# Four estimates of the issue planner change in a one-core RWKV-7 / Conformer inference step

## The chip, the cores and the metric

The kernel runs on one core of one Trainium2 chip. The metric is the device time of one execution in microseconds (us), lower is better. A core has five engines, each with its own list of instructions that it takes in order: TensorE (PE in the profile; PEld are its weight loads), VectorE (DVE), ScalarE (ACT), GpSimd (POOL) and SyncE (SP), which here issues the DMA transfers between HBM and the on-chip memory.

## The reference

One layer over 512 latent tokens and 128 context tokens with 1024 channels, all in float32. What is computed, cut to its core:

```python
mod = silu(cond) @ ada_w + ada_b                # 6 x 1024 columns, for the two conditions c and c_ctx
sh1, sc1, g1, sh2, sc2, g2 = split(mod, 6)
xn = rmsnorm(x, norm1_g) * (1 + sc1) + sh1
rkv, glu_in, gate_r, gate_c = split(xn @ w_in)  # 1536 + 1024 + 1024 + 1024 columns
y_r = rwkv7(rkv, xn)       # 8 heads, a forward and a backward scan over the tokens,
                           # plus bonus = sum(r * kd * r_k) * v, group norm, gate, @ w_out_rwkv
y_c = conv_branch(glu_in)  # GLU, depthwise conv of width 31, LayerNorm, swish, @ w_out_conv
merged = sigmoid(gate_r) * y_r + sigmoid(gate_c) * y_c
x = x + g1 * (merged @ w_o)
xn2 = rmsnorm(x, norm2_g) * (1 + sc2) + sh2
x = x + g2 * (relu(xn2 @ mlp_w1) ** 2 @ mlp_w2)
y = rmsnorm(x, final_g)    # also returned: the context's final scan states
```

## The kernel before

All 640 tokens lie along the free dimension, the channels on the 128 partitions. Every dense product is split in three: weights and activations are each held as a high and a low part in a 32-bit format that TensorE multiplies fast, and `mm3` adds high x high, high x low and low x high. The weights come as float32 blocks of 256 KB; ScalarE makes the high part, GpSimd (or VectorE) the low part.

The kernel has three stages. A set-up makes the modulation columns 0 to 15 (shift and scale of the first norm), the first norm and the low-rank inner products; it takes the first 55 us. Then comes one long stage, up to somewhat past 700 us, in which everything between the two norms is interleaved: the projections, the scans, the convolution, the gates and the branch outputs, and the modulation columns 16 to 47, called late here. The last stage is `w_o`, the second norm and the MLP.

The order in the long stage is planned while the program is built. Each strand of work is a Python generator, a lane: `solve`, `scan`, `side` and `prep` for each of four pairs of heads, the weight splitter, `lora2_all`, `ada_all`, `conv_all` and others. Each has an urgency in `URGENT`. A clock `now` runs on the estimated time of TensorE; `free` holds the estimated time at which VectorE, ScalarE and GpSimd are through with what has been issued. Their instructions go through `Timed`, which adds an estimate made by `cost_v`, `cost_a` or `cost_g`, and notes the estimated end in `last`. A lane runs until it yields. A number means: wake me so many microseconds of planned time from now. Nothing (or "T") means: wake me 0.2 us (`SEM`) after the estimated end of what I issued last. A letter means: wake me when that engine is nearly free. Whenever no lane may run, the filler issues one more dense product (`fill`, from the list `todo`). What comes out is a fixed order for TensorE, VectorE and ScalarE; the order of DMAs on SyncE and of instructions on GpSimd is set by the framework's own scheduler, which goes by its own timeline and issues what is ready.

The places that the change touches:

- `ada_late` and `ada` make one late column of the modulation: 1024 x 128 weights come in two halves of 256 KB into one buffer (`adl`, a single one, allocated in `adl_load`, L620). `ada_late` yields `GAP_ADA`, `ada` multiplies the first half (four products on bank `ad`), yields the pause in question, multiplies the second half, and two small products and two ScalarE instructions end the column. As there is one buffer, the second load can start only when the products of the first half have read it. `ada_all` goes through 32 columns with the urgency 4, next to the last. The pause is also used in the set-up, by the early columns.
- `root` raises a statistic to the power -0.5 on GpSimd; `inv_norm` calls it and then, on a plain yield, multiplies the result out on TensorE. In the long stage that is eight times with 10 columns (twice for each pair of heads) and twice with 3.
- `inverse` transposes 128 x 1024 elements in 32 x 32 blocks on VectorE, three times for each pair of heads; TensorE's products on the second and third result follow.
- `operands` ends with two VectorE instructions that leave the operand of the bonus in `kk`; the lane then marks the pair as prepared, and `side` calls `bonus`, whose products (`bsum`, bank `t`) read `kk`.

`calm` is an empty list during the set-up and holds one element from then on.

Of the kernel before, what the change touches and what calls it, by code (L numbers as in the profile page):

```python
# [13 lines left out]
ALU = mybir.AluOpType  # L14
# [46 lines left out]
LEAD, SEM, LOAD = 0.40, 0.2, 4.0  # L61
# [1 line left out]

URGENT = dict(scan=0, split=0.3, shift=1.45, post=1, side=0.9, solve=1, prep=1.5, lora=2, ada=4, out=4.5, branch=0.5, conv=1.6)

GAP_LORA, GAP_ADA = 1.5, 3.5
V_STEP = 20
GLU_AT = 12
TICK, ENTRY, QUOTA, CREDIT, STAY, DEBT = 3.413, 3060, 1.55, 700, 350, 6000
# [7 lines left out]
def hybrid_step(ctx: ExitStack, tc: tile.TileContext, I, O):  # L77
# [32 lines left out]
    def aps_(kw, *names):  # L110
        return sum(hasattr(kw.get(k), "shape") for k in names)

    def cost_v(name, n, src, kw):
        return 0.07 + 0.06 * aps_(kw, "scalar", "scalar1") + n / (480 if name == "tensor_tensor_scan" else 960)

    def cost_a(name, n, src, kw):
        return (0.08 if src[0].space == PSUM else 0.16) + 0.093 * aps_(kw, "scale", "bias") + n / 1400

    def cost_g(name, n, src, kw):
        return 1.9 if kw.get("op") == ALU.pow else 0.26 + n / (450 if name == "tensor_tensor" else 960)  # L120

    V, A, G = Timed(nc.vector, "V", cost_v), Timed(nc.scalar, "A", cost_a), Timed(nc.gpsimd, "G", cost_g)

# [6 lines left out]
    def bank(tag="mm"):  # L130
        return pp.tile([P, 512], F32, name="ps_" + tag, tag=tag, bufs=2 if tag == "mm" else 1)

    def st(shape, tag, bufs=1, dt=F32):
        return sb.tile(shape, dt, name=tag + "_t", tag=tag, bufs=bufs)
# [4 lines left out]
    def wt(shape, tag, bufs=1, dt=F32):  # L139
        return wk.tile(shape, dt, name=tag + "_w", tag=tag, bufs=bufs)  # L140

    def ldtmp():
        pool, n, cols = tmp_pool[-1]
        return pool.tile([P, cols], F32, name="tmp", tag="tmp", bufs=n)
# [16 lines left out]
    def pc(name, i, n=1):  # L161
        return par[:, PCOL[name] + i:PCOL[name] + i + n]
# [29 lines left out]
    def mm(out, lhsT, rhs, start=True, stop=True, **kw):  # L192
        PE.matmul(out=out, lhsT=lhsT, rhs=rhs, start=start, stop=stop, **kw)  # L193
        cyc = math.prod(rhs.shape[1:]) * (1 if rhs.dtype == F32R else 2 if "is_transpose" in kw else 4)
        m = math.prod(lhsT.shape[1:])
        overlap = 128 // m if m < 128 else 128 // rhs.shape[0]
        cols = cyc * rhs.shape[0] / 128 * (1 if rhs.dtype == F32R else 0.5)
        gated["cols"] += cols
        gated["burst"] -= cols
        gated["credit"] = min(gated["credit"] + cols, CREDIT)  # L200
        kind = (m, rhs.shape[0], rhs.dtype)
        if kind != gated["kind"]:
            advance(now[0] + SWITCH * gated["drain"] / (2400 if gated["warm"] else 1200))
        gated.update(kind=kind, drain=0 if rhs.dtype == F32R else max(cyc, 256) - max(cyc / overlap, 64))
        advance(now[0] + (max(cyc / overlap, 64) + EXTRA) / (2400 if gated["warm"] else 1200))
        ready[out.name] = ("P", now[0] + SEM / 2)
        last[0] = now[0]
# [7 lines left out]
    planner, calm = [lambda: None], []  # L215
# [142 lines left out]
    def inv_norm(src, scale, op, c, tg, bc):  # L358


        ps = bank(tg[0])
        for i in range(5):
            mm(ps[:, 2 * i:2 * i + 2], src[:, P * i:P * i + P], hsel)
        r = st([P, 10], "rh", 2)
        root(r, ps[:, 0:10], scale, op, c)
        yield
        for tag, a, b in ((tg[1], 0, 4), (tg[2], 4, 5)):
            pb = bank(tag)
            for i in range(a, b):
                for j in range(2):  # L370
                    mm(pb[64 * j:64 * j + 64, P * (i - a):P * (i - a) + P], r[:, 2 * i + j:2 * i + j + 1].to_broadcast([P, 64]),
                       ident)
            bc(P * a, P * b, pb[:, 0:P * (b - a)])
# [9 lines left out]
    def ada(cols, tag, raws):  # L383

        n = len(cols) * P
        ps = bank(tag)
        for k0, k1, raw in raws:
            for k in range(k0, k1):
                g = 32 * (k % 4)
                mm(ps[g:g + 32, 0:n], csb[:, 2 * k:2 * k + 32], raw[:, k - k0, :], k < 4, k >= 4, tile_position=(0, g))  # L390
            yield 2.5 if k0 == 0 else 0.0
        e = ldtmp()[:, 0:n]
        A.activation(e, ps[:, 0:n], AF.Copy)
        yield
        for i, col in enumerate(cols):
            mm(ps[:, n + 2 * i:n + 2 * i + 2], e[:, i * P:(i + 1) * P], sel)
        for i, col in enumerate(cols):
            A.activation(mod[:, col, :], ps[:, n + 2 * i:n + 2 * i + 2], AF.Identity, bias=pc("ada_b", col))
# [113 lines left out]
    def dram(name):  # L512
        if name not in spill:
            spill[name] = dr.tile([P, T], F32, name=name, tag=name)
        return spill[name]
# [146 lines left out]
    def operands(p):  # L662

        gr = grp[p]
        gr["Dc"] = wt([P, NY], "Dc", 2)
        r, k = rk[0, p], rk[1, p]

        def load(d):
            th, at = st([P, T], "tA"), st([P, T], f"ath{d}")
            DMA.dma_start(out=th, in_=dram(f"z0{d}{p}"))  # L670
            DMA.dma_start(out=at, in_=dram(f"z1{d}{p}"))
            return th, at

        loaded = load(0)
        t0 = st([P, T], "pt0")
        A.activation(t0, k, AF.Square, scale=pc("k_k", p))
        kk = gr["kk"] = st([P, T], "kk")
        yield
        yield from inv_norm(t0, 1.0, "max", 1e-24, ("t",) * 3,
                            lambda a, b, ps: V.scalar_tensor_tensor(out=kk[:, a:b], in0=k[:, a:b], scalar=pc("k_k", p),  # L680
                                                                    in1=ps, op0=ALU.mult, op1=ALU.mult))
        ath = []
        for d in range(2):
            ys = slice(20 * d, 20 * d + 20)

            def tv(ap):
                return (ap[:, ::-1] if d else ap).rearrange("p (y t) -> p y t", t=C32)


            th, at = loaded  # L690
            ath.append(at)
            A.activation(th, th, AF.Copy, bias=1.0)
            yield "T"
            cs = st([P, 20, C32], "tB")
            csf = cs.rearrange("p y t -> p (y t)")
            for a, b in HALVES:
                V.tensor_tensor_scan(out=csf[:, a:b], data0=smask, data1=th[:, a:b], initial=0.0,
                                     op0=ALU.mult, op1=ALU.add)
                yield "V"
            if d == 0:  # L700
                loaded = load(1)
            yield "T"
            A.activation(E[:, :, 1:33], cs, AF.Exp, scale=-0.5 * CDEC)
            yield "A"
            A.activation(cs, cs, AF.Exp, scale=0.5 * CDEC)
            yield "A"
            if d == 0:
                while p and (3 not in rates or (p > 1 and p - 2 not in chained)):
                    yield 0.2
                ARGH = gr["ARGH"] = st([P, 2, NY, 64], "ARGH", 2)  # L710
            A.activation(gr["Dc"][:, ys].unsqueeze(2), E[:, :, 32:33], AF.Copy)
            V.tensor_tensor(out=ARGH[:, 0, ys, 0:32], in0=tv(kk), in1=E[:, :, 0:32], op=ALU.mult)
            yield "V"
            V.tensor_tensor(out=ARGH[:, 0, ys, 32:64], in0=tv(r), in1=E[:, :, 1:33], op=ALU.mult)
            DMA.dma_start(out=ARGH[64:128, 1, ys, :], in_=ARGH[64:128, 0, ys, :])
            yield "V"
            if d == 0:
                while p and turned[p - 1] < 3:
                    yield 0.2
                BK = gr["BK"] = wt([P, NY, 64], "BK")  # L720
            bc, kc = (0, 32) if d == 0 else (32, 0)
            t1 = st([P, T], "pt0")
            V.scalar_tensor_tensor(out=t1, in0=at, scalar=1.0, in1=kk, op0=ALU.add, op1=ALU.mult)
            yield "V"
            V.scalar_tensor_tensor(out=BK[:, ys, bc:bc + 32], in0=tv(t1), scalar=-0.5, in1=cs,
                                   op0=ALU.mult, op1=ALU.mult)
            yield "A"
            A.activation(at, at, AF.Identity, scale=ka2[:, p:p + 1], bias=ka2[:, 4 + p:5 + p])
            yield "T"
            V.tensor_tensor(out=at, in0=at, in1=k, op=ALU.mult)  # L730
            yield "V"
            V.tensor_tensor(out=BK[:, ys, kc:kc + 32], in0=tv(at), in1=cs, op=ALU.mult)
            yield "V"
        operated.add(p)
        V.tensor_tensor(out=kk, in0=ath[0], in1=ath[1], op=ALU.add)
        yield "V"
        V.scalar_tensor_tensor(out=kk, in0=kk, scalar=pc("r_k", p), in1=r, op0=ALU.mult, op1=ALU.mult)
        yield SEM

    BKt = wt([P, 2, NY, 64], "BKt")  # L740
    for s in range(2):
# [908 lines left out]
```

## Time and profile before

| | |
|---|---|
| median of 3 runs | 1296.28 us (1286.36 to 1297.65) |
| the profiled execution | 1300.42 us, its span 1298.6 us |
| TensorE busy | 1228.2 us, 95% of the span |
| VectorE, ScalarE, GpSimd busy | 56%, 42%, 12% |
| mean granted TensorE clock | 0.958 of full speed |
| moved by DMA | 140.43 MB, mean 108 GB/s |

The span reaches from the first to the last instruction of the profiled execution; 1.8 us of its time lie outside. TensorE's busy share counts time in which products run, at whatever clock; matmuls are pipelined and their ends are modelled. [...]

### The profile page before, as it was taken

To read this page: it belongs to the slowest core of one execution; us is meant where nothing else is said; L and a number is where in the kernel's file an instruction comes from. 1 tells how busy PE (TensorE), PEld (TensorE's weight loads), DVE (VectorE), ACT (ScalarE), POOL (GpSimd) and SP (SyncE) were. 2 spreads that over 40 slices of the span, in tenths; PEclk is the share of its full clock that TensorE was granted. 3 is DMA by queue.
4 is the path that set the end of the run, shared out by engine and by line. 5 is a ranking of instruction groups with operands and counts; after the bars stand their busy time and mean duration, and the time that the engine had idled before them with its cause. 6 is when DMAs were issued, how large, how long until landed. Compare 5 with 4: busy or idle time off the path is not lost.

```text
span 1298.6 us, 31716 instructions
## 1 busy us (share of the span) xinstructions
PE 1228.2 (95%) x13362; PEld 1092.9 (84%) x13362; DVE 720.9 (56%) x1446; ACT 548.8 (42%) x1390; POOL 152.4 (12%) x112
## 2 busy tenths in 40 slices
PE   8988899998999899999979999999999999999996
PEld 5776676777677776777979999999999999999996
DVE  5525576747557766877953365664433443444344
ACT  5545466634555565465225123354421431342130
POOL 1122120112011100122413310000000000000000
PEclk9998999968799989999989999999999999999998
DMA  9445433113222522343413853112222222222222
GB/s 370 151 158 175 143 109 114 59 43 119 77 94 68 153 92 70 116 126 93 136 58 121 270 195 125 49 50 82 72 75 81 67 82 74 74 82 69 78 74 82
DMA packets 82575, 140.43 MB, mean 108 GB/s; under 512 B 17024, under 2 KB 31616, under 8 KB 82432
## 3 DMA queue, kind: packets, MB, share of 16 engines
q1 hardware_dynamic: 82432, 138.39, 33.2%
q8 instruction: 105, 1.72, 0.6%
q14 instruction: 38, 0.31, 0.1%
HBM read 113.52 MB, written 22.22 MB: 105 GB/s over the span
## 4 chain that ended last, share of the span: by engine, by line
PE 82%; DVE 7%; DMA 6%; issue 2%; ACT 1%; SPq 0%; POOL 0%; POOLq 0%; DVEq 0%; ACTq 0%
PE ps_mm L193 43%; PE ps_b L193 24%; PE ps_t L193 7%; PE ps_a L193 6%; DMA adl_w<-in_adal 3%; PE ps_ad L193 3%; DVE BK_w L106 2%; DVE cacc_w L106 1%; DMA adar_s<-in_adaw 1%; DVE vS_w L106 1%; DVE ARGH_t L106 1%; DMA u_t<-gate 1%; DMA svu_w<-in_st 0%; DVE kk_t L106 0%; DVE svu_w L106 0%
## 5 line engine op out<-in xcount | busy, mean ns | idle before, releaser
L193 PE MATMUL ps_mm<-xh_t,wh_t 128*128 128x320 f32 x584 | 198.2, 339 | 0.9 <-ACT tmp L106 0.9
L193 PE MATMUL ps_mm<-xh_t,wl_t 128*128 128x320 f32 x584 | 198.8, 340 | 0.0
L193 PE MATMUL ps_mm<-xl_t,wh_t 128*128 128x320 f32 x584 | 196.7, 337 | 0.0
L106 ACT ACTIVATE wh_t<-wr_t 128x512 fp32r<-128x512 f32 x135 | 84.9, 629 | 143.2 <-PE ps_b L193 108.4
L106 POOL TENSOR_TENSOR wl_t<-wr_t,wh_t 128x512 fp32r<-128x512 f32 x63 | 85.0, 1350 | 462.0 <-ACT wh_t L106 418.0
L106 ACT ACTIVATE svu_w<-ps_a 64x128 f32<-64x128 f32 x320 | 87.0, 272 | 122.9 <-PE ps_a L193 117.3
L193 PEld LDWEIGHTS ps_mm<-xh_t,wl_t 128*128 128x128 f32 x584 | 117.0, 200 | 10.8 <-issue 7.2
L193 PEld LDWEIGHTS ps_mm<-xl_t,wh_t 128*128 128x128 f32 x584 | 116.7, 200 | 9.6 <-issue 6.1
L193 PEld LDWEIGHTS ps_mm<-xh_t,wh_t 128*128 128x128 f32 x584 | 116.3, 199 | 9.6 <-issue 4.3
L106 DVE SCALAR_TENSOR_TENSOR cacc_w<-upad_w,par_t,cacc_w 128x640 f32<-128x640 f32 x90 | 88.6, 984 | 4.3 <-ACT cacc_w L106 2.1
L106 DVE TENSOR_TENSOR wl_t<-wr_t,wh_t 128x512 fp32r<-128x512 f32 x72 | 49.7, 690 | 56.2 <-ACT wh_t L106 56.2
L106 ACT ACTIVATE tmp<-ps_mm 128x320 f32<-128x320 f32 x80 | 34.9, 436 | 98.9 <-PE ps_mm L193 90.4
L193 PE MATMUL ps_mm<-ARGH_t,wh_t 128*128 128x320 f32 x284 | 74.8, 308 | 0.0
L106 DVE TENSOR_TENSOR svu_w<-ps_b,Dc_w 64x128 f32<-64x128 f32 x152 | 43.7, 288 | 54.5 <-PE ps_b L193 51.0
L106 POOL TENSOR_TENSOR rt_t<-rt_t,mhalf_t 128x3 f32<-128x3 f32 (+1 forms) x7 | 6.5, 921 | 532.0 <-DVE rt_t L106 532.0
L193 PE MATMUL ps_mm<-ARGH_t,wl_t 128*128 128x320 f32 x212 | 65.8, 310 | 0.0
L106 ACT ACTIVATE mwh<-wr_t 128x512 fp32r<-128x512 f32 x49 | 31.0, 632 | 71.1 <-PE ps_b L193 66.8
L106 DVE SCALAR_TENSOR_TENSOR ARGH_t<-ps_mm,mod_t,ARGH_t 128x320 f32<-128x320 f32 (+2 forms) x45 | 22.6, 511 | 59.9 <-PE ps_mm L193 59.9
L106 DVE TENSOR_TENSOR tmp<-tmp 128x320 f32<-128x320 f32 x64 | 31.2, 489 | 43.8 <-ACT tmp L106 43.7
L106 DVE TENSOR_TENSOR mwl<-wr_t,mwh 128x512 fp32r<-128x512 f32 x49 | 33.8, 690 | 34.9 <-ACT mwh L106 34.9
L193 PEld LDWEIGHTS ps_mm<-ARGH_t,wh_t 128*128 128x128 f32 x284 | 50.4, 188 | 0.0
L106 ACT ACTIVATE BKt_w<-ps_a 32x512 f32<-32x512 f32 (+3 forms) x80 | 39.9, 503 | 19.9 <-PE ps_a L193 18.9
(372 smaller groups left out, 3226.2 us busy)
## 6 DMA issues: line engine op xcount, KB each, us to landing
wr_t<-in_w SPq DMA_DIRECT2D x214, 256.0 KB, 2.7
adl_w<-in_adal SPq DMA_DIRECT2D x64, 256.0 KB, 3.0
adar_s<-in_adaw SPq DMA_DIRECT2D x16, 512.0 KB, 8.4
ARGH_t<-in_x SPq DMA_DIRECT2D x8, 640.0 KB, 6.9
z<-tmp SPq DMA_DIRECT2D x32, 160.0 KB, 3.0
gate<-tmp SPq DMA_DIRECT2D x32, 160.0 KB, 2.2
tA_t<-z SPq DMA_DIRECT2D x8, 320.0 KB, 3.1
ath_t<-z SPq DMA_DIRECT2D x8, 320.0 KB, 3.3
```

The source lines that it names most:

```text
L106: return f(*args, **kw)
L193: PE.matmul(out=out, lhsT=lhsT, rhs=rhs, start=start, stop=stop, **kw)
```

## The change

Four estimates of the planner change; every instruction and every operand stays. `GAP_ADA` goes from 3.5 to 4.5, and the pause between the two halves of a late column, 2.5 before, becomes `GAP_ADA` too (in the set-up it stays 2.5). A block transpose on VectorE is counted with 520 elements per microsecond in place of 960, a power on GpSimd with 2.6 us in place of 1.9. At the end of `operands` the lane yields nothing in place of `SEM`: it wakes 0.2 us after the estimated end of its last instruction, not 0.2 us after issuing it.

```diff
-GAP_LORA, GAP_ADA = 1.5, 3.5
+GAP_LORA, GAP_ADA = 1.5, 4.5
@@ cost_v
-        return 0.07 + 0.06 * aps_(kw, "scalar", "scalar1") + n / (480 if name == "tensor_tensor_scan" else 960)
+        return 0.07 + 0.06 * aps_(kw, "scalar", "scalar1") + n / (480 if name == "tensor_tensor_scan" else 520 if name == "transpose" else 960)
@@ cost_g
-        return 1.9 if kw.get("op") == ALU.pow else 0.26 + n / (450 if name == "tensor_tensor" else 960)
+        return 2.6 if kw.get("op") == ALU.pow else 0.26 + n / (450 if name == "tensor_tensor" else 960)
@@ ada
-            yield 2.5 if k0 == 0 else 0.0
+            yield (GAP_ADA if calm else 2.5) if k0 == 0 else 0.0
@@ operands
         V.scalar_tensor_tensor(out=kk, in0=kk, scalar=pc("r_k", p), in1=r, op0=ALU.mult, op1=ALU.mult)
-        yield SEM
+        yield
```

## Rows read from the trace of the kernel before

**Rows 1.** The page's busy times: us (share of the span) xinstructions.
```profile
PE 1228.2 (95%) x13362; PEld 1092.9 (84%) x13362; DVE 720.9 (56%) x1446; ACT 548.8 (42%) x1390; POOL 152.4 (12%) x112
```

**Rows 2.** TensorE's waits, whole span: us in total, times, longest.
```profile
PE ps_ad L193 <- DMA adl_w<-in_adal: 17.0, 9, 2.9
PE ps_t L193 <- DVE kk_t L106: 7.5, 8, 1.8
```

**Rows 3.** The waits of TensorE's weight loads, whole span.
```profile
PEld ps_ad L193 <- DMA adl_w<-in_adal: 19.5, 10, 3.1
```

**Rows 4.** Timeline (start, us; in brackets the idle before): the five longest such waits.
```profile
64.72 0.16 PEld L193 LDWEIGHTS ps_ad<-adl_w,csb_t 128*32 128x32 f32 x8 [2.33 <-DMA adl_w<-in_adal]
77.62 0.20 PEld L193 LDWEIGHTS ps_ad<-adl_w,csb_t 128*32 128x32 f32 x8 [2.81 <-DMA adl_w<-in_adal]
112.00 0.20 PEld L193 LDWEIGHTS ps_ad<-adl_w,csb_t 128*32 128x32 f32 x8 [2.55 <-DMA adl_w<-in_adal]
328.03 0.20 PEld L193 LDWEIGHTS ps_ad<-adl_w,csb_t 128*32 128x32 f32 x8 [3.14 <-DMA adl_w<-in_adal]
454.82 0.16 PEld L193 LDWEIGHTS ps_ad<-adl_w,csb_t 128*32 128x32 f32 x8 [2.28 <-DMA adl_w<-in_adal]
```

**Rows 5.** Timeline: first halves and SyncE's loads behind them; the lane's last product.
```profile
59.67 0.16 PEld L193 LDWEIGHTS ps_ad<-adl_w,csb_t 128*32 128x32 f32 x8 [0.18 <-issue]
60.59 0.45 SPq L620 DMA_DIRECT2D adl_w<-in_adal  x1
...
321.29 0.16 PEld L193 LDWEIGHTS ps_ad<-adl_w,csb_t 128*32 128x32 f32 x8
324.64 0.81 SPq L620 DMA_DIRECT2D adl_w<-in_adal  x1
...
552.17 0.16 PEld L193 LDWEIGHTS ps_ad<-adl_w,csb_t 128*32 128x32 f32 x8
```

**Rows 6.** SyncE's waits, whole span: us in total, times, longest.
```profile
SPq L620 <- PE ps_ad L193: 102.7, 36, 8.9
```

**Rows 7.** Stretches: us, busy of five engines (instructions), granted clock, DMA share, GB/s.
```profile
76.00:84.00 8.00, 6.38 (x37) 5.32 (x38) 0.00 (x0) 3.32 (x9) 1.34 (x2) 0.79 0.41 132
112.00:124.00 12.00, 11.33 (x55) 9.14 (x56) 6.24 (x9) 5.19 (x12) 1.35 (x1) 0.58 0.32 102
144.00:152.00 8.00, 6.94 (x76) 5.17 (x77) 4.95 (x7) 2.37 (x8) 0.00 (x0) 0.79 0.24 83
...
324.00:344.00 20.00, 17.12 (x189) 13.31 (x189) 8.99 (x17) 8.63 (x27) 2.60 (x2) 0.57 0.27 74
456.00:464.00 8.00, 8.00 (x137) 6.80 (x140) 5.39 (x12) 4.86 (x13) 0.00 (x0) 0.57 0.28 85
260.00:288.00 28.00, 26.02 (x271) 19.07 (x271) 13.39 (x52) 9.68 (x25) 3.23 (x2) 0.57 0.12 39
```

**Rows 8.** The chain that ended last: runs of dense products, start, us, count.
```profile
118.08 5.37 PE ps_mm L193 x21
...
775.67 3.52 PE ps_mm L193 x24
```

**Rows 9.** Timeline: a slower power and the products that read it.
```profile
540.83 2.52 POOL L106 TENSOR_TENSOR rh_t<-rh_t,mhalf_t 128x10 f32<-128x10 f32 x1 [3.25 <-DVE rh_t L106]
544.10 0.85 PEld L193 LDWEIGHTS ps_t<-cst_t,rh_t 128*64 128x64 f32 x16
```

**Rows 10.** Timeline: a block transpose and the products on its result.
```profile
168.84 2.21 DVE L106 STREAM_TRANSPOSE Gt_w<-Nb_w 128x1024 f32<-128x1024 f32 x1
171.97 0.76 PEld L193 LDWEIGHTS ps_t<-Gt_w,Gf_w 32*32 32x32 f32 x80 [0.19 <-issue]
```

**Rows 11.** Timeline: the bonus's operand and the products on it.
```profile
219.04 0.88 DVE L106 SCALAR_TENSOR_TENSOR kk_t<-kk_t,par_t,rS_w 128x640 f32<-128x640 f32 x1
220.75 0.20 PEld L193 LDWEIGHTS ps_t<-kk_t,cst_t 128*64 128x64 f32 x4 [0.73 <-ACT Y_w L106]
```

**Rows 12.** Timeline: the store of the last gate.
```profile
711.50 0.38 SPq L611 DMA_DIRECT2D gate<-tmp  x1
```

## The prediction

> **What bounds the kernel now.** I read the page's busy shares first: TensorE works 95% of the span [rows 1], so its instruction list, which it takes strictly in order, is what the time is made of. A changed order can bring time in two ways only: less idling between products, or a higher granted clock while they run.
>
> Second, the waits by engine: of what TensorE waited for, the largest item is the late modulation's weight load, 17.0 us in 9 waits; next come waits on VectorE's kk, 7.5 us in 8 [rows 2]. The same loads seen from the weight-load side are 19.5 us in 10 waits [rows 3]. The reader should see that these stalls are few and long and belong to one lane.
>
> Third, the timeline at those waits: the five longest (2.28 to 3.14 us) stand in [rows 4]. Each is at the second half of a column: the column at 59.67 multiplies its first half, its second load is issued at 60.59 when the one buffer is free, and the second half starts at 64.72 after 2.33 us of nothing [rows 4, 5]. The planner put 2.5 us between the halves; the load took 4.13 us from issue to product. At 321.29 it was worse: the first half's products ran, and SyncE came to the next load only at 324.64 [rows 5]. So 2.5 us is too little for two reasons, the transfer and the queue ahead of it.
>
> Fourth, the granted clock by stretch [rows 7]. Right behind six of the late loads the mean clock is 0.57 to 0.79, though TensorE is busy again. [...] The six stretches (a third of the 0.79 kind, 196 to 204, is like the two shown) give 3.4 + 10.1 + 3.4 + 3.4 + 17.2 + 6.9 = 44.4 us at half clock. Another, 260 to 288, has 24.1 us of it and no late load: half clock has other causes too.
>
> **The change, part by part.** No instruction is added or removed; only the place of instructions in the lists of TensorE, VectorE and ScalarE moves, and with them the places that SyncE's and GpSimd's own instructions find.
>
> *Gap between the halves, 2.5 to 4.5 us.* It puts 2 us more of other products between the halves of each of 32 columns. The load does not move with it: it is issued when the buffer is free (60.59, less than a microsecond after the products at 59.67 began [rows 5]), not when the lane wakes. So every wait shrinks by 2 us. Of the five listed, 0.33 + 0.81 + 0.55 + 1.14 + 0.28 = 3.1 us stay; the other five waits together are 19.5 - 13.1 = 6.4 us, 1.3 on average, and I take them as gone. Removed: 16.4 of 19.5 us on the weight-load side; on TensorE's own account the same share of 17.0 us, 14.3 us. Bounds: nothing, if SyncE comes to the load later by the same 2 us, and 17.0 us.
>
> *Gap before a column, 3.5 to 4.5 us.* All late loads belong to second halves, so this removes no wait: 0. Together the two gaps make the lane up to 32 x 3.0 = 96 us longer. Its last product load is at 552.17 [rows 5]; it would end by about 650. Cover: dense gate products run until the last gate is stored at 711.50 [rows 12], so no engine waits for the lane, and its results are first read after the loop. If that cover is gone, a column alone costs about 13 us, as between the second halves of the first two columns, at 64.72 and 77.62 [rows 4].
>
> *SyncE behind the load.* While SyncE stands at such a load for the buffer it can issue nothing else: 102.7 us in 36 waits already [rows 6]. Queued behind are weight loads, for which ScalarE and GpSimd would wait and then TensorE. None of that reaches TensorE today (no such row among its waits), and the blocking depends on when the first half ends, not on the gap. I take 0; the bound on the other side is that weights come late as often as the modulation's did, 17.0 us [rows 2], which takes the first gap's gain away again.
>
> *GpSimd's power, 1.9 to 2.6 us.* It moves the products that read the power 0.7 us later, eight times. One of the slower powers took 2.52 us, ended at 543.35, and its products came at 544.10 with no wait noted [rows 9]. So there is nothing to remove: 0, bounds 0 and plus or minus 8 x 0.7 = 5.6 us if the cover of dense products failed.
>
> *Block transposes, 1.14 to 2.04 us as planned.* The trace has 2.21 us for the one at 168.84, and TensorE's products on its result, at 171.97, show 0.19 us of ordinary issue time [rows 10]. No wait to remove: 0. The planner will think VectorE busy 0.9 us longer, 12 times, and place up to 10.8 us of other VectorE work later; VectorE is at 56% [rows 1], so that is the bound against the change, and I take 0.
>
> *End of the bonus's operand.* The lane now wakes when the operand is done and not 0.2 us after it was issued. At 219.04 the operand took 0.88 us, to 219.92; TensorE's product on it came at 220.75 after 0.73 us of waiting, put down to ScalarE's reading of the shared bank [rows 11]. The operand was done before that wait began, so I take 0; bounds 0 and 4 x 0.88 = 3.5 us. The 7.5 us of kk waits [rows 2] are mostly the second use of one bank by the same lane without a pause, which stays.
>
> *The clock.* The same kind of dense product comes every 3.52 / 24 = 0.147 us at full clock and every 5.37 / 21 = 0.256 us in the half-clock stretch behind the wait at 112.00 [rows 8]. So a microsecond at half clock loses 1 - 0.147/0.256 = 0.43 us, and the 44.4 us lose 19.0 us. How much comes back the rows don't settle: six late loads have such a stretch behind them, four have none, and 260 to 288 fell without one [rows 7]. Between 0 and 19.0 us I take the middle, 9.5 us.
>
> [...]
>
> The sum goes against the profiled execution: span 1298.6, time 1300.4 us, which is 4.1 us above the median of the runs shown (1286.4 to 1297.7). 1300.4 - 14.3 - 9.5 = 1276.6, so 1277 us, 1.5% under the median.
>
> **The rivals.**
>
> *The clock is not won back.* The late loads go, but the clock falls at other places of the new order. For it: 24.1 us at half clock with no late load. Against it: six of the late loads are followed by it directly. Time: 1300.4 - 14.3 = 1286.
>
> *The load stays as late.* SyncE reaches the load 2 us later because the order ahead of it has grown. For it: 324.64 [rows 5]. Against it: 60.59, at once when the buffer was free. Time: 1300, no change; with the clock's spread 1291 to 1301.
>
> [...]
>
> *Slower: half clock during a scan.* Moving modulation columns to later places leaves the scan's small products with less beside them, and the clock stays at half as from 260 to 288, which lies in the first scan. Price 0.43 us per us; three more stretches like that one (72 us at half clock) cost 31 us: 1286 + 31 = 1317. It decides for slower when the loss passes 1309 - 1286 = 23 us, that is 54 us more at half clock than the profiled run has without its late loads. For it: that stretch exists. Against it: nothing in the change touches the scan's own gaps.
>
> *Slower: the lane outlasts the loop.* It would have to slip 160 us, to beyond 711.50; the gaps give at most 96. Each column left over costs 13 us, so two of them decide.
>
> **How the numbers follow.** A measurement of this kernel can tell about 1% from no change: 1283 to 1309 counts as the same. Forecast (1264 to 1283, waits gone and part of the clock back): 0.55. Clock not won back (1283 to 1291): 0.18. Load as late as before (1291 to 1301): 0.12. Half clock in a scan: 0.12, lane outlasts the loop: 0.03, both above 1309. Hence faster 0.55, same 0.30, slower 0.15. The likeliest case's own range is 1264 (all 36.0 us of both terms) to 1283. The range to hold 8 in 10 reaches down to 1260, since other runs shown lie up to 14 us under the profiled one, and up to 1301, where 0.15 is left out above and some 0.05 below.
>
> **What would show it.** Right: waits on the late modulation's weights under 4 us in total; its last product between 580 and 650; mean clock from 55 to 560 higher, with no half-clock stretch behind a modulation product; kk waits still near 7.5 us; the tail after 711 only shifted. Wrong: SyncE issuing second-half loads later than the buffer is free; half clock at stretches without any wait; waits on weights (wr) at TensorE.

## The result, and the profile after

| | before | after |
|---|---|---|
| median of the runs taken side by side | 1293.99 us | 1253.48 us (1248.87 to 1256.57) |
| ratio after / before | | 0.969, 95% interval 0.963 to 0.975 |
| the profiled execution, its span | 1300.42, 1298.6 us | 1256.57, 1254.8 us |
| TensorE busy | 1228.2 us | 1203.8 us |
| idle (span less busy) | 70.4 us | 51.0 us |
| mean granted clock | 0.958 | 0.985 |

The change is faster by 3.1%, where 1.5% was forecast; the time lies below the range of 1260 to 1301 us. Of the 43.8 us between the two spans, 19.4 are idle time and 24.4 are time in which TensorE is busy. The products are the same in number, so the second part is speed. The granted clocks give another split. In steps of 1 us the clock of before reads 1.00 of full speed in 1176 steps, 0.50 in 94 and a value between in 28, each of these at a change from one to the other; after reads 1.00 in 1206, 0.50 in 31 and between in 17. With these two levels, (1 - clock) x 2 x span gives 109 us of the one span and 38 of the other at half clock, 71 x 0.43 = 30.5 us by the price from [rows 8], and 13.3 us are the rest. The ends of products are modelled, so the two splits need not agree closely.

The page's busy times, which answer [rows 1], as us (share of the span) xinstructions:

```profile
PE 1203.8 (96%) x13362; PEld 1071.6 (85%) x13362; DVE 720.5 (57%) x1446; ACT 547.7 (44%) x1390; POOL 152.8 (12%) x112
```

TensorE's waits after, to hold against [rows 2] (us in total, times, longest):

```profile
PE ps_t L193 <- DVE kk_t L106: 7.0, 9, 1.1
PE ps_t L193 <- DVE vS_w L106: 5.9, 7, 1.4
...
PE ps_ad L193 <- DMA adl_w<-in_adal: 0.5, 1, 0.5
```

The late modulation's wait is down from 17.0 to 0.5 us, and the waits on kk have stayed. The timeline of the first column, the counterpart of [rows 4, 5], shows how:

```profile
64.92 0.16 PEld L193 LDWEIGHTS ps_ad<-adl_w,csb_t 128*32 128x32 f32 x8 [0.44 <-issue]
65.95 0.42 SPq L620 DMA_DIRECT2D adl_w<-in_adal  x1
71.07 0.16 PEld L193 LDWEIGHTS ps_ad<-adl_w,csb_t 128*32 128x32 f32 x8 [0.19 <-issue]
...
631.47 0.20 PEld L193 LDWEIGHTS ps_ad<-adl_w,csb_t 128*32 128x32 f32 x8 [0.33 <-issue]
```

The second load still goes out when the buffer is free, 1.03 us after the first half began; the second half comes 6.15 us after the first and finds its weights there. Before it came 5.05 us after it, of which 2.33 were idle. In the other columns it is the same: after, 29 of the 32 second loads are issued within 0.5 us of the end of the first half's products, the latest 1.44 us behind it. The lane's last product is at 631.47, after 552.17 before. SyncE's standing at these loads [rows 6] went from 102.7 to 66.2 us:

```profile
SPq L620 <- PE ps_ad L193: 66.2, 27, 8.4
```

The granted clock by stretch, in the columns of [rows 7], the kernel after:

```profile
55.00:560.00 505.00, 483.51 (x8277) 383.13 (x8276) 339.96 (x714) 292.96 (x853) 98.13 (x68) 0.99 0.38 116
```

and before:

```profile
55.00:560.00 505.00, 465.33 (x7815) 362.75 (x7816) 313.45 (x672) 270.67 (x786) 82.15 (x56) 0.92 0.36 109
```

From 55 to 560 us the clock is full but for about 10 us at half (505 x 0.01 x 2), where before had 81 (505 x 0.08 x 2). That is more than the 44.4 us counted behind the late loads. So the question for the experiments is where the rest of the clock came from.

**How the runs are split below.** Each run comes with its span and mean granted clock, so two numbers can be worked out of it: the time at half clock, (1 - clock) x 2 x span, and a remainder, the span less 0.43 us for each us at half clock (the price from [rows 8]). Over the 52 runs of before that were taken beside the experiments, 1277.9 to 1317.7 us, the time at half clock goes from 59 to 155 us, while the remainder stays between 1247 and 1255 us. Nearly all of what one kernel's runs differ by is thus clock, and the remainder, which holds the idle time and the work at full clock, belongs to the order. Taken the other way, the spans of these 52 runs rise by 0.40 us per us at half clock, near that price. In the table are the runs within about 1.5% of the fastest of their kernel; slower ones, at a lower granted clock (12 of the 52 of before, one each of r1, r8 and r9), are left out.

| kernel | median, us | ratio to before, 95% | wait on late loads in its profile, us | half clock a run, mean (least to most), us | remainder, mean, us |
|---|---|---|---|---|---|
| before | 1286.0 | | 17.0 | 78 (59 to 104) | 1251.8 |
| after | 1253.5 | 0.963 to 0.975 | 0.5 | 31 (23 to 38) | 1238.1 |
| r1 second loads left out | 1265.9 | 0.976 to 0.994 | 1.2 | 62 (53 to 76) | 1238.3 |
| r2 pause between halves | 1268.0 | 0.978 to 0.992 | 7.3 | 50 (38 to 66) | 1245.5 |
| r3 three costs | 1256.2 | 0.969 to 0.983 | 6.5 | 50 (40 to 71) | 1234.6 |
| r4 pause before a column | 1271.5 | 0.981 to 0.993 | 7.1 | 60 (53 to 71) | 1244.2 |
| r5 after, eight loads slowed | 1264.5 | 0.978 to 0.989 | 6.1 | 51 (45 to 56) | 1240.9 |
| r6 unrelated edit | 1277.3 | 0.987 to 0.995 | 14.7 | 66 (43 to 77) | 1247.5 |
| r7 unrelated edit | 1271.5 | 0.982 to 0.997 | 16.4 | 55 (46 to 64) | 1246.3 |
| r8 unrelated edit | 1280.7 | 0.990 to 0.999 | 14.8 | 69 (48 to 88) | 1248.3 |
| r9 both pauses | 1281.8 | 0.996 to 1.001 | 0.8 | 90 (79 to 105) | 1240.8 |
| r10 transposes | 1267.1 | 0.985 to 0.989 | 10.7 | 49 (46 to 51) | 1244.4 |
| r11 power | 1262.3 | 0.981 to 0.987 | 8.9 | 50 (45 to 58) | 1240.4 |
| r12 end of the operand | 1265.2 | 0.981 to 0.989 | 11.6 | 48 (35 to 58) | 1242.2 |
| r13 after, unrelated edit | 1267.8 | 0.976 to 0.997 | 1.2 | 63 (56 to 79) | 1241.6 |
| r14 after, unrelated edit | 1259.7 | 0.963 to 0.989 | 0.3 | 60 (35 to 78) | 1229.6 |
| r15 both pauses, unrelated edit | 1258.2 | 0.969 to 0.986 | 0 | 49 (43 to 58) | 1236.0 |
| r16 both pauses, unrelated edit | 1269.8 | 0.978 to 0.995 | 2.2 | 70 (66 to 79) | 1238.7 |
| r17 after, pause at bank t | 1244.1 | 0.964 to 0.972 | 0 | 35 (22 to 42) | 1226.2 |
| r18 the same in another order | 1236.5 | 0.960 to 0.969 | 0.2 | 27 (20 to 35) | 1223.8 |

The ratio of each kernel is to the runs of before on its own chip and at its own time; the first row is over all of them. Beside r1 to r4 before had 84 us at half clock on average, beside r5 to r8 83, beside r9 to r12 68, beside r13 to r18 77. The waits, and every place named below, are those of one profiled execution of each kernel; that of before has 109 us at half clock, more than any run in its row.

### The profile page after: what moved, and what is told of

Read it like the earlier page. It is cut to its first block, busy times and chain, and to the rows that moved or that the text cites. A ratio compares the mean times of both kernels' runs of the same rounds, so it can differ in the third digit from the quotient of the medians.

```text
span 1254.8 us, 31737 instructions
## 1 busy us (share of the span) xinstructions
PE 1203.8 (96%) x13362; PEld 1071.6 (85%) x13362; DVE 720.5 (57%) x1446; ACT 547.7 (44%) x1390; POOL 152.8 (12%) x112
## 4 chain that ended last, share of the span: by engine, by line
PE 85%; DVE 6%; DMA 3%; ACT 2%; issue 2%; SPq 0%; POOL 0%; POOLq 0%; DVEq 0%; ACTq 0%
PE ps_mm L193 44%; PE ps_b L193 25%; PE ps_a L193 7%; PE ps_t L193 7%; PE ps_ad L193 3%; DVE BK_w L106 2%; DVE ARGH_t L106 1%; DVE vS_w L106 1%; DMA kS_w<-gate 0%; ACT svu_w L106 0%; DVE kk_t L106 0%; DMA ARGH_t<-in_x 0%; DMA u_t<-gate 0%; ACT tmp L106 0%; DMA mr<-rS_w 0%
## 5 line engine op out<-in xcount | busy, mean ns | idle before, releaser
L193 PE MATMUL ps_mm<-xh_t,wh_t 128*128 128x320 f32 x608 | 201.2, 331 | 2.1 <-ACT tmp L106 2.1
L106 ACT ACTIVATE wh_t<-wr_t 128x512 fp32r<-128x512 f32 x140 | 87.8, 628 | 134.4 <-PE ps_b L193 107.9
L106 POOL TENSOR_TENSOR wl_t<-wr_t,wh_t 128x512 fp32r<-128x512 f32 x68 | 93.6, 1378 | 429.4 <-ACT wh_t L106 363.0
L106 DVE SCALAR_TENSOR_TENSOR cacc_w<-upad_w,par_t,cacc_w 128x640 f32<-128x640 f32 x90 | 85.9, 955 | 5.3 <-ACT cacc_w L106 3.0
L106 DVE TENSOR_TENSOR svu_w<-ps_b,Dc_w 64x128 f32<-64x128 f32 x152 | 43.8, 288 | 37.4 <-PE ps_b L193 34.0
```

Of the source, the lines that this page charges most:

```text
L106: return f(*args, **kw)
```

## The experiments

### The late loads alone, in the old order

```diff
-            raw = wt([P, KD // 2, P], "adl")
-            DMA.dma_start(out=raw, in_=I["adal"][col - 16, :, 4 * j:4 * j + 4, :])
+            raw = raw if j else wt([P, KD // 2, P], "adl")
+            j or DMA.dma_start(out=raw, in_=I["adal"][col - 16, :, 4 * j:4 * j + 4, :])
```

> The kernel before, with the load of the second half of each late modulation column left out; its products read the first half's weights again, so TensorE's, VectorE's, ScalarE's and GpSimd's lists are those of the kernel before, instruction by instruction, and only 32 loads of 256 KB are missing. Theory A (the late loads cost their idle time and the half clock right behind them, the rest of the half clock has other causes): 17.0 us of waits and 19.0 us of clock go, 1258 to 1264 us, and the half clock around 260 to 288 us stays. Theory B (the new order itself keeps the clock up, the loads cost their idle time alone): 1275 to 1280 us, with half clock elsewhere in the old order. Theory C (one late load sets later stalls and clock drops off too): 1245 to 1256 us, with the clock full nearly everywhere from 55 to 560 us.

1265.9 us, 1.5% under before. The remainder falls from 1251.8 to 1238.3: 13.5 us went, with no instruction of TensorE, VectorE or ScalarE in another place. In the profiled execution the clock is now full at the products of all six stretches that [rows 7] place behind a late load. Two of them, before at 112 to 124 and at 324 to 344 (by the second r1 is 21 us ahead):

```profile
112.00:124.00 12.00, 10.29 (x123) 8.12 (x121) 9.53 (x12) 6.26 (x15) 2.62 (x2) 1.00 0.64 190
303.00:314.00 11.00, 11.00 (x197) 8.60 (x197) 9.24 (x17) 8.48 (x28) 2.12 (x2) 1.00 0.35 93
```

So the half clock behind these late loads, 44.4 us in the profiled execution of before, is caused by them; that much of theory A holds. As theory A has it, too, the stretch at 260 to 288 stays, 17 us at half clock (26 x 0.33 x 2) where it had 24:

```profile
245.00:271.00 26.00, 24.02 (x276) 18.29 (x276) 13.04 (x51) 10.24 (x26) 3.23 (x2) 0.67 0.10 32
```

But over the runs the time at half clock fell only from the 84 us of before beside it to 62 us, not by 44. The profiled execution of before was one with much half clock, that of r1 (53 us) the one with least of its row; how much of the 44.4 us a usual run of before has, no trace shows.

Theories A and C both asked for more clock than came back, and theory B for none: the time lies between A's 1264 and B's 1275.

### The edits one by one

The pause between the halves:

```diff
-            yield 2.5 if k0 == 0 else 0.0
+            yield (4.5 if calm else 2.5) if k0 == 0 else 0.0
```

> The kernel before with one edit of the change alone: the pause between the halves of a late column 4.5 in place of 2.5, the pause before a column 3.5 as before, all cost estimates as before. Theory A and C: nearly the whole gain, 1250 to 1268 us, waits on the late modulation's weights under 4 us. Theory B: the gain hangs on the exact order, so this may land anywhere from 1255 to 1290 us.

The two costs and the end of the operand, as in the change:

```diff
-    ... n / (480 if name == "tensor_tensor_scan" else 960)
+    ... n / (480 if name == "tensor_tensor_scan" else 520 if name == "transpose" else 960)
-        return 1.9 if kw.get("op") == ALU.pow else ...
+        return 2.6 if kw.get("op") == ALU.pow else ...
-        yield SEM
+        yield
```

> The kernel before with the three other edits alone: the transposes' and the power's estimates and the end of the bonus's operand; both pauses as before. Theory A and C: no wait is removed, waits on the late modulation's weights stay at 12 to 22 us, 1285 to 1300 us. Theory B: the order is another one throughout, so 1265 to 1310 us, with the clock and not the waits making the difference.

The pause before a column:

```diff
-GAP_LORA, GAP_ADA = 1.5, 3.5
+GAP_LORA, GAP_ADA = 1.5, 4.5
```

> The kernel before with the pause before a column 4.5 in place of 3.5 alone, the pause between the halves 2.5 as before. Theory A and C: no late load is covered by it, waits on the late modulation's weights stay at 12 to 22 us, 1285 to 1300 us. Theory B: anywhere from 1265 to 1310 us.

All three come out faster, 1268.0, 1256.2 and 1271.5 us, with intervals below 1. For theories A and C only the first should have been. The pause between the halves does not clear the late loads by itself either, 7.3 us stay where under 4 were expected. The longest of them, 3.4 us, stands behind a load that SyncE issued 2.6 us after the first half's products had ended, and whose own products began 6.3 us behind the issue. And the two edits that were to leave the loads alone have 6.5 and 7.1 us of them in place of 17.0. An edit anywhere in these estimates moves everything behind it: from the first row that differs to the last, at some 790 to 860 us, TensorE's list has another tile in 67% of the rows (the changed kernel) to 81% (r3). That the three costs alone bring almost the whole gain was in no theory; even B's range began at 1265.

### Late loads put back into the new order

```diff
+            for _ in range(2 if j and col - 16 in (0, 1, 4, 6, 9, 10, 17, 25) else 1):
-            DMA.dma_start(out=raw, in_=I["adal"][col - 16, :, 4 * j:4 * j + 4, :])
+                DMA.dma_start(out=raw, in_=I["adal"][col - 16, :, 4 * j:4 * j + 4, :])
```

> The changed kernel with the second half's load of eight late columns (the ones whose load was late before: 0, 1, 4, 6, 9, 10, 17, 25) issued twice into the same buffer, so that these loads end some 3 us later; TensorE's order is that of the changed kernel but for four rows. Theory A (a late load costs its idle time and half clock behind it, in any order): 8 waits of 1 to 3 us come back, 8 to 20 us of idling and 10 to 20 us of clock, 1270 to 1292 us. Theory B (the late loads matter only by their idle time, the clock is a matter of the order): 1261 to 1272 us with the mean clock still near 0.985.

1264.5 us, 11.0 over the changed kernel, which was not run beside it. TensorE's waits on the loads:

```profile
PE ps_ad L193 <- DMA adl_w<-in_adal: 6.1, 4, 2.9
```

Three of the eight came late, and one short wait is at a column that was not slowed. Two waits are long, and half clock stands right behind both; more of it stands at 630 to 656, where no load is late any more (the last late one is at 430):

```profile
86.20 0.20 PEld L193 LDWEIGHTS ps_ad<-adl_w,csb_t 128*32 128x32 f32 x8 [2.79 <-DMA adl_w<-in_adal]
133.40 0.16 PEld L193 LDWEIGHTS ps_ad<-adl_w,csb_t 128*32 128x32 f32 x8 [3.37 <-DMA adl_w<-in_adal]
...
86.00:93.00 7.00, 6.79 (x30) 5.22 (x31) 0.88 (x2) 2.09 (x5) 0.00 (x0) 0.52 0.45 150
134.00:138.00 4.00, 4.00 (x55) 3.48 (x50) 0.85 (x2) 1.60 (x6) 0.00 (x0) 0.57 0.41 119
630.00:656.00 26.00, 22.41 (x106) 19.37 (x105) 10.48 (x20) 6.60 (x16) 0.85 (x1) 0.67 0.10 35
```

The remainder rose by 2.8 us and the half clock from 31 to 51 us, 8.6 us at 0.43. In the profiled execution some 10 us (7 x 0.48 x 2 + 4 x 0.43 x 2) are directly behind the two late loads; the 17 us at 630 to 656, where the changed kernel has 7 (628 to 660), are not. So a late load costs its idle time and half clock behind it in this order too, as theory A has it, but the whole rise can't be put down to it. The time lies in theory B's range and under theory A's, with two long waits where eight were meant.

### Orders drawn by unrelated edits

```diff
-GAP_LORA, GAP_ADA = 1.5, 3.5
+GAP_LORA, GAP_ADA = 1.7, 3.5
```

> The kernel before with an edit that has nothing to do with the change: the pause behind the low-rank products 1.7 in place of 1.5. It corrects no estimate and aims at no wait, but the order becomes another one throughout. Theory D (any new order is better than the one before, which was an unfortunate draw): 1255 to 1275 us. Theory E (the three corrected costs work by what they correct): 1280 to 1300 us, with late loads as before.

```diff
-LEAD, SEM, LOAD = 0.40, 0.2, 4.0
+LEAD, SEM, LOAD = 0.45, 0.2, 4.0
```

> The kernel before with another unrelated edit: LEAD, by how much a lane may run ahead of an engine that is nearly free, 0.45 in place of 0.40. Theory D: 1255 to 1275 us. Theory E: 1280 to 1300 us.

```diff
-            yield 2.5 if n == 3 else None
+            yield 2.6 if n == 3 else None
```

> The kernel before with a third unrelated edit: the scan's pause for the loaded state, after its fourth step, 2.6 in place of 2.5. Theory D: 1255 to 1275 us. Theory E: 1280 to 1300 us.

1277.3, 1271.5 and 1280.7 us: the first lies between the two theories' ranges, the second in D's, the third in E's. The late loads are nearly all there (14.7 to 16.4 us) and the remainder is nearly that of before, 1246 to 1248. What is better is the clock, 55 to 69 us at half where before beside them has 83. Against these three the order of before was a poor draw for the clock, by some 14 to 28 us of half clock, 6 to 12 us of time.

### Both pauses, and each cost alone

```diff
-GAP_LORA, GAP_ADA = 1.5, 3.5
+GAP_LORA, GAP_ADA = 1.5, 4.5
-            yield 2.5 if k0 == 0 else 0.0
+            yield (4.5 if calm else 2.5) if k0 == 0 else 0.0
```

> The kernel before with both pauses of the late modulation at 4.5 and all three other edits left out. Theory D (the gain is the late loads, plus an order that is not the unfortunate one of before; the costs add nothing): 1250 to 1262 us, late loads under 4 us. Theory E (the corrected costs add a gain of their own): 1263 to 1275 us, 10 us or more above the changed kernel.

```diff
-    ... n / (480 if name == "tensor_tensor_scan" else 960)
+    ... n / (480 if name == "tensor_tensor_scan" else 520 if name == "transpose" else 960)
```

> The kernel before with the transposes' estimate alone corrected. Theory D: like the three unrelated edits, 1268 to 1284 us with 14 to 17 us of late loads. Theory E, if the transposes are what works in the three costs: 1250 to 1262 us.

```diff
-        return 1.9 if kw.get("op") == ALU.pow else ...
+        return 2.6 if kw.get("op") == ALU.pow else ...
```

> The kernel before with the power's estimate on GpSimd alone corrected. Theory D: 1268 to 1284 us with 14 to 17 us of late loads. Theory E, if the power is what works in the three costs: 1250 to 1262 us.

```diff
-        yield SEM
+        yield
```

> The kernel before with the end of the bonus's operand alone changed. Theory D: 1268 to 1284 us with 14 to 17 us of late loads. Theory E, if this edit is what works in the three costs: 1250 to 1262 us.

Both pauses without the costs do what they are for, and gain nothing that shows: the wait on the late loads is 0.8 us, the remainder 1240.8, 11 us under before, and yet the time is 1281.8 us, above the ranges of both theories, since 79 to 105 us a run are at half clock, where before beside it has 68. Its profiled execution, with 143 us, shows the longest such stretch of all the profiles (the columns of [rows 7]); it tells what half clock looks like, and not how much of it the median run has:

```profile
582.00:633.00 51.00, 51.00 (x439) 37.37 (x435) 19.57 (x49) 16.59 (x58) 5.07 (x4) 0.50 0.25 80
```

For 51 us TensorE is busy without a gap at a granted clock of 0.50. The longest idle time in the 8 us ahead is this one, on its weight load:

```profile
580.05 0.41 PEld L193 LDWEIGHTS ps_a<-svu_w,ARGH_t 128*32 128x32 f32 x8 [1.41 <-ACT wh_t L106]
```

What it works on inside, by shape (busy us, mean ns), are small products of the last scan, which ends at 629 us here, with dense products between them; the largest group of each:

```profile
L193 PE MATMUL ps_mm<-xh_t,Gf_w 128*128 128x320 f32 x16 | 7.5, 521 | 0.0
L193 PE MATMUL ps_b<-svu_w,BKt_w 128*64 128x64 f32 x72 | 6.3, 328 | 0.0
```

This is the rival "half clock during a scan", near its price (51 x 0.43 = 22 us), mainly in the last scan (14 us more are in the first), and without the costs. It is not the only one. In ten of the twenty profiled executions a stretch of 17 us or more at half clock overlaps one of the four scans and follows no late load: in before, r1, r2, r3, r4, r8, r9, r11, r14 and r16, that is in orders with and without the pauses and with and without the costs. Here the 8 us ahead of the one of before and that stretch itself, and then the one of r3, in which the three costs alone are changed:

```profile
254.00:262.00 8.00, 7.58 (x128) 6.10 (x128) 6.32 (x13) 5.49 (x15) 1.27 (x1) 1.00 0.21 67
262.00:286.00 24.00, 22.43 (x223) 16.22 (x223) 9.47 (x46) 7.02 (x19) 3.23 (x2) 0.50 0.10 34
...
247.00:281.00 34.00, 32.48 (x329) 22.71 (x328) 13.80 (x34) 8.22 (x27) 3.22 (x2) 0.50 0.13 42
```

The changed kernel, r5, r6, r7, r10, r12, r13, r15, r17 and r18 have none of that length in their profiles. The ten executions with one have 54 to 142 us at half clock in all, the ten without 20 to 73. What brings such a stretch on, no run here shows. Behind the late loads r1 shows a cause (without these loads 0.58 and 0.57 became 1.00), while none of these stretches follows a late load.

Each of the three costs alone gives 1262 to 1267 us, between the ranges of the two theories, with 8.9 to 11.6 us of late loads left and 48 to 50 us of half clock. Against before beside them that is 1.3 to 1.6% less, where the unrelated edits gave 0.6 to 1.1%: some 8 us better. The clock does not show as the reason, since the half clock fell as much here (by 19 us on average) as there (by 20); the remainder is 5 us lower. That two explanations were still open then (the costs keep the clock up, or every order has a clock of its own) led to the next runs.

### The changed kernel's neighbours

The unrelated edits of r6 and r7, on the changed kernel (r13, r14) and on the two pauses alone (r15, r16).

```diff
-GAP_LORA, GAP_ADA = 1.5, 4.5
+GAP_LORA, GAP_ADA = 1.7, 4.5
```

> The changed kernel with the unrelated edit of the pause behind the low-rank products, 1.7 in place of 1.5. Theory E (corrected costs keep the clock up): 1248 to 1262 us, half clock 20 to 45 us a run. Theory F (half clock is a matter of the exact order): 1255 to 1280 us, half clock anywhere from 30 to 90 us.

> The kernel with the two pauses alone (r9) and the unrelated edit of the pause behind the low-rank products, 1.7 in place of 1.5. Theory E: 1272 to 1290 us, half clock 70 to 110 us a run, since the costs are not corrected. Theory F: 1250 to 1275 us, half clock anywhere from 30 to 90 us; r9 itself is an unfortunate order.

```diff
-LEAD, SEM, LOAD = 0.40, 0.2, 4.0
+LEAD, SEM, LOAD = 0.45, 0.2, 4.0
```

> The changed kernel with the unrelated edit LEAD 0.45 in place of 0.40. Theory E: 1248 to 1262 us, half clock 20 to 45 us a run. Theory F: 1255 to 1280 us, half clock anywhere from 30 to 90 us.

> The kernel with the two pauses alone (r9) and the unrelated edit LEAD 0.45 in place of 0.40. Theory E: 1272 to 1290 us, half clock 70 to 110 us a run. Theory F: 1250 to 1275 us, half clock anywhere from 30 to 90 us.

With the costs 1267.8 and 1259.7 us at 63 and 60 us of half clock, without them 1258.2 and 1269.8 at 49 and 70. Of half clock theory E asked for 20 to 45 us and for 70 to 110. Both pairs spread over one range, as theory F has it. So the 31 us of the changed kernel are a good draw, as the 90 of r9 and the 78 of before are poor ones. The remainder, on the other hand, goes with the pauses: 1229.6 to 1241.6 in the six kernels that have both and no further edit at the loads or at the banks, 1246 to 1252 in before and the three unrelated edits. It goes with the waiting that is left, 0.7 us for each us on late loads by a straight line through the table's rows from before to r16. But r3, which has neither pause, and r14 lie 7 us under that line, for which no run shows a reason.

### A pause at bank t

The waits on kk and vS left in the changed kernel come at bank `t`, used twice by one lane without a pause. A plain yield between the two uses:

```diff
             bc(P * a, P * b, pb[:, 0:P * (b - a)])
+            yield
...
             if NY3 and h == 0:
-                yield 0.0
+                yield
```

> The changed kernel with a plain yield behind the first use of bank t in inv_norm and in bsum, so that the second use is issued when VectorE or ScalarE is through with the first and other products stand between. If the waits on kk and vS on this bank (7.0 + 5.9 us) go: the span less 0.43 us per us of half clock falls from 1238 to some 1227 us. The time itself hangs on the clock of the new order: 1240 to 1265 us.

and, in addition:

```diff
-LEAD, SEM, LOAD = 0.40, 0.2, 4.0
+LEAD, SEM, LOAD = 0.45, 0.2, 4.0
```

> The same edit with LEAD 0.45 in place of 0.40, that is in another order. The span less 0.43 us per us of half clock, 1230 us without the pause (r14), falls to some 1219 us if the bank's waits go. Time 1232 to 1260 us, by the clock of the order.

1244.1 and 1236.5 us, ratios to before 0.968 and 0.964. All runs of both are faster than the fastest of the changed kernel, 1248.9 us; but they were not taken beside it, and by its ratio to before r17 is no better (0.969). What tells them apart is the remainder. In r17 those waits are nearly gone:

```profile
PE ps_t L193 <- DVE kk_t L106: 0.9, 2, 0.6
PE ps_t L193 <- DVE vS_w L106: 0.7, 1, 0.7
```

The remainder fell from 1238.1 to 1226.2, by 11.9 us, where 11 was expected. In r18 it fell from 1229.6 to 1223.8, 5.8 in place of 11, although the two waits went from 15.2 to 3.7 us. The rest of r18's gain over r14 is clock again, 27 us at half in place of 60.

## Why the prediction was wrong

**Right: the waits.** The term of 14.3 us for the late loads is what the remainder shows, 13.7 us from before to after, and r1 takes away 13.5 with the order untouched. That the changed kernel meets it so closely is luck in part: r13 and r14, with the same pauses and waits as short, lie 10 and 22 us under before. The waits left were to be under 4 us and are 0.5; the lane was to end between 580 and 650 and ends at 631.47; the load was to go out when the buffer is free, and does; no weights (wr) come late at TensorE; the waits on kk stayed near 7.5, at 7.0. It was right for the pauses taken together. That "every wait shrinks by 2 us" was too simple: with the one pause alone 7.3 us stay (r2), since the column's products and SyncE's issue have moved as well.

**Wrong: the clock's term, in its size and its bounds.** The step was "between 0 and 19.0 us I take the middle, 9.5 us". The 44.4 us under it take the clock to be full or half and nothing else, which none of the rows beside them shows; the steps of 1 us in the traces of before and after do. Measured are (109 - 38) x 0.43 = 30.5 us between the two profiled executions (the sum started from the one of before) and (78 - 31) x 0.43 = 20 us between the rows of the table; both are above the upper bound. The price per us at half clock was about right, 0.43 (0.40 by the runs; the half-clock run of products in [rows 8] has its last 1.45 of 5.37 us, from 122.0 on, at full clock, so 0.43 is read a little low there). Wrong was to let the term reach only to the 44.4 us behind the late loads and to leave everything else at half clock standing, the 24.1 us at 260 to 288 among it. All of it is drawn anew with the order, and the changed kernel's order has no such stretch. Of the 47 us less at half clock some are the loads' doing: r1 has 21 less than before beside it in the old order, and in the new one r5 has some 10 directly behind two late loads. The others are the draw, in which the long stretches over a scan weigh most (17 to 51 us each). In kernels whose late loads are gone, 27 to 90 us of half clock have been measured.

**Wrong in kind: the run it was reckoned from.** The profiled execution's 109 us at half clock (1298.6 x 0.042 x 2) was above the 78 of the table. The sum started from one draw of the old order and took no account of what the other runs shown, 14 us apart, already said of the clock. The range's lower end, 4 us under "all 36.0 us of both terms", should have taken the whole half clock into its bounds: 109 x 0.43 = 47 us, not 19.

**The edits priced at 0.** Each of the three costs alone made the kernel 1.3 to 1.6% faster, which 0 did not foresee; no wait on the eight powers or on a transpose was there to remove, and none is named as removed now; the waits on kk are 8.2, 8.0 and 5.3 us, where before has 7.5. Part of the gain is the draw and fewer late loads (8.9 to 11.6 us left). Whether a corrected cost also brings something by what it corrects stays open: three costs together have the remainder 1234.6 with 6.5 us of late loads, as low as orders without late loads, but r13 to r16 show no difference with and without them beyond the spread.

**The rivals.** "Half clock during a scan" had 0.12 for the change. The changed kernel's profile has no such stretch; but r14, the same kernel with one unrelated edit, has one of 24 us, and r9 one of 51. In r9 half clock ate the whole gain of the pauses, in the other runs too, of which no trace shows where it stood. That nothing in the change touches the scan's own gaps was thus no argument: the order around them changes. "The clock is not won back" and "the load stays as late" are refuted for the changed kernel by its clock and its waits. The lane did not outlast the loop: the last gate is stored at 663 us.

## What to carry to other kernels

Where a change draws the whole order anew, split each run into time at half clock and the remainder before explaining anything: the remainder could be forecast to some 10 us here, the time at half clock varied from 27 to 90 us between orders and from 59 to 155 us between runs of before. One changed kernel against one unchanged one then tells little about an edit; two or three unrelated edits beside it show how wide the draw is, and an experiment that keeps the order (leaving a load out, slowing one down) shows what the edit's own cause is worth. The bound of a clock term is all the time at half clock, not the part that stands behind the wait in question.

## What the runs showed of the hardware

TensorE's granted clock fell from 1.00 to 0.50 without a wait above 1.41 us in the 8 us ahead of it and stayed there for 51 us while TensorE was busy for all of the 51 us, on small products of the scan and dense ones in turn (r9, 582 to 633). In before it fell at 262, after 8 us of which TensorE was busy for 7.58, and stayed for 24 us. The kernel before spent between 59 and 155 us a run at that level, and its time followed at 0.40 us per us (0.43 by the dense products of [rows 8]). Late loads of 256 KB can bring half clock behind them: with the same lists and without these loads the 44.4 us behind six of them were gone (r1), and two late ones put into another order had some 10 us behind them (r5). Four of the ten waits of before, one of 2.33 us among them, had none.
